# Row softmax on one Trainium2 core: two pairs of input chunks loaded as one DMA each

## The chip, the core and the metric

The kernel runs on one core of a Trainium2 chip. Of the core's engines it uses VectorE (DVE in the profile) for maxima, reciprocals and most of the scaling, ScalarE (ACT) for exponentials and the rest of the scaling, and the 16 DMA engines that move data between HBM and the core's on-chip memory (SBUF, 128 partitions). SyncE (SP) issues the loads and ScalarE's queue issues the stores. The metric is the device time of one execution in microseconds; the kernel before takes 162.3 us (median of 3 runs, 162.19 to 162.3).

## The reference

A softmax over rows of 512 numbers, with temperature 0.5, on 16 x 1024 = 16384 rows of float32 (33.55 MB in, 33.55 MB out):

```python
x_scaled = x / 0.5
x_max = np.max(x_scaled, axis=-1, keepdims=True)
exp_x = np.exp(x_scaled - x_max)
return exp_x / np.sum(exp_x, axis=-1, keepdims=True)
```

## The kernel before

The rows are cut into C = 8 chunks of 2048 rows. In a chunk each of the 128 partitions holds G = 16 consecutive rows, so a chunk is 4 MiB and one partition's part of it is 32 KiB, contiguous in HBM. Everything is done in place in a chunk's tile `xt`. There are six tiles (`BUFS = 6`); chunks 6 and 7 reuse the tiles of chunks 0 and 1.

`load(c)` (line 66) issues a chunk's loads on SyncE. Chunk 0 is loaded as two DMAs, 4 rows a partition and then 12; the others are one DMA each (`LOADS`). The first seven DMAs (chunks 0 to 5) need no free tile and are issued at once; those of chunks 6 and 7 wait until the stores of chunks 0 and 1 have landed. Loads are called from `shift`, but SyncE's own order is simply chunk order.

The compute works on blocks (`BLOCKS`): chunk 0 in three blocks of 4, 4 and 8 rows a partition, chunks 1 to 6 as one block of 16 each, chunk 7 as two of 8; eleven blocks in all. For each block:

- `shift(i)`: VectorE takes the negated maximum of every row (line 74, `negmax`) and doubles it (line 78, `bias`). Line 74 is the first instruction that needs the block's load to have landed.
- `exponentials(i, rows)`: ScalarE computes exp(2x + bias) row by row, with the row's sum (line 86).
- `scale_vector(i)`: VectorE takes the reciprocals of the sums (line 101) and multiplies the first 7/8 of the rows (line 103).
- `scale_scalar(i)`: ScalarE multiplies the remaining rows (line 112).
- `store(i)`: after a chunk's last block, ScalarE issues one DMA for the whole chunk (line 120).

The order on each engine is the program's (`manual_schedule`); nothing is rearranged. The main loop is short:

```python
    for i in range(n):
        if i + 1 < n:
            exponentials(i + 1, rows(i + 1)[0])
        scale_vector(i)
        scale_scalar(i)
        if i + 2 < n:
            shift(i + 2)
        store(i)
        if i + 1 < n:
            exponentials(i + 1, rows(i + 1)[1])
```

On VectorE this makes the sequence: scaling of block i, maximum of block i+2, scaling of block i+1, maximum of block i+3. The maximum of chunk 2 (block 4) thus stands ahead of the scaling of chunk 1 (block 3), whichever is ready first. On ScalarE the store of block i stands after the exponentials of block i+1.

Of the kernel before, what the change touches and what calls it, by code (L numbers as in the profile page):

```python
# [1 line left out]

# [4 lines left out]


@with_exitstack
def kernel(  # L10
    ctx: ExitStack,
    tc: tile.TileContext,
    x: bass.AP,
    out: bass.AP,
):
    nc = tc.nc
    fp32 = mybir.dt.float32
    P = nc.NUM_PARTITIONS
    AX = mybir.AxisListType.X
    EXP = mybir.ActivationFunctionType.Exp  # L20
    COPY = mybir.ActivationFunctionType.Copy
    MAX = mybir.AluOpType.max

    D = x.shape[-1]
    xf = x.flatten_outer_dims()
    of = out.flatten_outer_dims()
    N = xf.shape[0]

    G = 16
    C = N // (P * G)
    assert C * P * G == N
    xr = xf.rearrange("(c p g) d -> c p g d", p=P, g=G)
    outr = of.rearrange("(c p g) d -> c p g d", p=P, g=G)
    WHOLE = [(0, G)]
    LOADS = [[(0, 4), (4, G)]] + [WHOLE] * 7
    BLOCKS = [[(0, 4), (4, 8), (8, G)]] + [WHOLE] * 6 + [[(0, 8), (8, G)]]
    STORES = [WHOLE] * 8  # L40
    BMAX = 16
    BUFS = 6

    data = ctx.enter_context(tc.tile_pool(name="data", bufs=BUFS))
    stats = ctx.enter_context(tc.tile_pool(name="stats", bufs=6))

    ctx.enter_context(tc.manual_schedule())


    warm = stats.tile([P, 1], fp32, name="warm", bufs=1)  # L50
    nc.vector.memset(warm, 0.0)  # L51
    nc.scalar.activation(out=warm, in_=warm, func=EXP)  # L52

    chunks = {}
    blocks = [(c, lo, hi) for c in range(C) for lo, hi in BLOCKS[c]]
    n = len(blocks)
    biases, sums, recips = {}, {}, {}

    def load(c):
        if c < BUFS:  # L60
            chunks[c] = data.tile([P, G, D], fp32, name="xt")
        else:
            chunks[c] = chunks[c - BUFS]
        xt = chunks[c]
        for lo, hi in LOADS[c]:
            nc.sync.dma_start(out=xt[:, lo:hi, :], in_=xr[c][:, lo:hi, :])  # L66

    def shift(i):
        c, lo, hi = blocks[i]
        if c not in chunks:  # L70
            load(c)
        b = hi - lo
        negmax = stats.tile([P, BMAX], fp32, name="negmax")
        nc.vector.tensor_reduce(  # L74
            negmax[:, 0:b], chunks[c][:, lo:hi, :], axis=AX, op=MAX, negate=True
        )
        biases[i] = stats.tile([P, BMAX], fp32, name="bias")
        nc.vector.tensor_scalar_mul(biases[i][:, 0:b], negmax[:, 0:b], 2.0)  # L78

    def exponentials(i, rows):  # L80
        c, lo, hi = blocks[i]
        if i not in sums:
            sums[i] = stats.tile([P, BMAX], fp32, name="sums")
        for g in rows:
            row = chunks[c][:, lo + g, :]
            nc.scalar.activation(  # L86
                out=row,
                in_=row,
                func=EXP,
                bias=biases[i][:, g : g + 1],  # L90
                scale=2.0,
                accum_out=sums[i][:, g : g + 1],
            )


    def scale_vector(i):
        c, lo, hi = blocks[i]
        b = hi - lo
        k = b - b // 8
        recips[i] = stats.tile([P, BMAX], fp32, name="recip")  # L100
        nc.vector.reciprocal(recips[i][:, 0:b], sums[i][:, 0:b])  # L101
        rows = chunks[c][:, lo : lo + k, :]
        nc.vector.tensor_mul(  # L103
            rows, rows, recips[i][:, 0:k].unsqueeze(2).broadcast_to((P, k, D))
        )

    def scale_scalar(i):
        c, lo, hi = blocks[i]
        b = hi - lo
        for g in range(b - b // 8, b):  # L110
            row = chunks[c][:, lo + g, :]
            nc.scalar.activation(  # L112
                out=row, in_=row, func=COPY, scale=recips[i][:, g : g + 1]
            )

    def store(i):
        c, _, end = blocks[i]
        for lo, hi in STORES[c]:
            if hi == end:
                nc.scalar.dma_start(  # L120
                    out=outr[c][:, lo:hi, :], in_=chunks[c][:, lo:hi, :]
                )

    shift(0)
    shift(1)

    def rows(i):
        c, lo, hi = blocks[i]
        cut = hi - lo - (2 if c == 1 else 0)
        return range(cut), range(cut, hi - lo)  # L130

    exponentials(0, rows(0)[0])
# [12 lines that stand above are left out]
# [1 line left out]
_INS = ['x']  # L146
_OUTS = [((16, 1024, 512), 'float32')]


# [23 lines left out]
```

## Time and profile before

| | |
|---|---|
| median of the runs | 162.3 us |
| profiled execution | 162.04 us |
| its span | 160.3 us |
| VectorE busy | 134.6 us (84%), 45 instructions |
| ScalarE busy | 102.2 us (64%), 273 instructions |
| HBM read, written | 33.55 MB, 33.55 MB; 419 GB/s over the span |
| maximum of a whole chunk (line 74) | 8.68 us |
| scaling of a whole chunk (line 103) | 7.62 us |
| chunk store, issue to landing | 22.8 us (median of 8) |
| whole-chunk load, issue to landing | 30.1 us (median of 7) |

A profile line of a group reads: line, engine, operation, output<-input, count, busy time, mean duration of one. In the timeline the first two numbers are start and duration in us; "SPq" and "ACTq" are DMA issues by SyncE and ScalarE. In the list of waits the numbers are total us, number of waits and the longest. In the page's slices each digit is the busy share, in tenths, of one fortieth of the span. A row of DMA issues ends with the size of one and the us from issue to landing. The row of a stretch gives the stretch, its length, the busy time (and instruction count) of VectorE, ScalarE and GpSimd, the TensorE clock (not used here), the DMA engines' busy share and GB/s.

### The profile page before, as it was taken

To read this page: it belongs to the slowest core of one execution; us is meant where nothing else is said; L and a number is where in the kernel's file an instruction comes from. 1 tells how busy PE (TensorE), PEld (TensorE's weight loads), DVE (VectorE), ACT (ScalarE), POOL (GpSimd) and SP (SyncE) were. 2 spreads that over 40 slices of the span, in tenths; PEclk is the share of its full clock that TensorE was granted. 3 is DMA by queue.
4 is the path that set the end of the run, shared out by engine and by line. 5 is a ranking of instruction groups with operands and counts; after the bars stand their busy time and mean duration, and the time that the engine had idled before them with its cause. 6 is when DMAs were issued, how large, how long until landed. Compare 5 with 4: busy or idle time off the path is not lost.

```text
span 160.3 us, 402 instructions
## 1 busy us (share of the span) xinstructions
DVE 134.6 (84%) x45; ACT 102.2 (64%) x273; POOL 0.2 (0%) x4
## 2 busy tenths in 40 slices
DVE  0607999999999999999999999999999999957000
ACT  3071549069989972998199909991899891690000
POOL 0000000000000000000000000000000000000000
DMA  5999999999999999999999999999999999999993
GB/s 180 474 409 491 409 401 483 425 393 452 458 393 401 393 425 474 409 393 499 417 393 474 442 393 468 442 393 442 474 393 417 491 401 401 491 417 401 466 442 139
DMA packets 2450, 67.13 MB, mean 419 GB/s; under 512 B 272, under 2 KB 272, under 8 KB 272
## 3 DMA queue, kind: packets, MB, share of 16 engines
q1 hardware_dynamic: 1296, 33.56, 49.4%
q10 hardware_dynamic: 1152, 33.55, 48.5%
q14 instruction: 2, 0.02, 0.0%
HBM read 33.55 MB, written 33.55 MB: 419 GB/s over the span
## 4 chain that ended last, share of the span: by engine, by line
DVE 80%; DMA 7%; ACT 4%; issue 0%; SPq 0%
DVE negmax L74 42%; DVE xt L103 36%; DMA xt<-in_x_dram 7%; ACT xt L86 4%; DVE bias L78 1%; DVE recip L101 1%; SPq L66 0%
## 5 line engine op out<-in xcount | busy, mean ns | idle before, releaser
L86 ACT ACTIVATE xt<-xt,bias 128x512 f32<-128x512 f32 x128 | 90.4, 708 | 41.5 <-DVE bias L78 40.6
L74 DVE TENSOR_REDUCE negmax<-xt 128x16 f32<-128x8192 f32 (+2 forms) x11 | 69.9, 6353 | 9.5 <-DMA xt<-in_x_dram 9.5
L103 DVE TENSOR_TENSOR xt<-xt,recip 128x7168 f32<-128x7168 f32 (+2 forms) x11 | 62.0, 5637 | 0.4
L86 ACT ACTIVATION_READ_ACCUMULATOR xt<-xt,bias 128x1 f32 x128 | 23.9, 187 | 0.0
L112 ACT ACTIVATE xt<-xt,recip 128x512 f32<-128x512 f32 x15 | 9.9, 707 | 0.0
L101 DVE RECIPROCAL recip<-sums 128x16 f32<-128x16 f32 (+2 forms) x11 | 2.4, 218 | 1.8 <-ACT xt L86 1.8
L78 DVE TENSOR_SCALAR bias<-negmax 128x16 f32<-128x16 f32 (+2 forms) x11 | 1.9, 173 | 0.4
L52 ACT ACT_TABLE_LOAD x1 | 1.3, 1283 | 0.7 <-PEq L157 0.7
L51 DVE MEMSET warm<- 128x1 f32 x1 | 0.1, 59 | 0.8 <-PEq L157 0.8
L52 ACT ACTIVATE warm<-warm 128x1 f32<-128x1 f32 x1 | 0.2, 202 | 0.0
L157 POOL MEMSET const-bfloat16-1.0<- 128x1 bf16 x1 | 0.1, 101 | 0.0
L157 POOL MEMSET const-uint8-127<- 128x1 uint8 x1 | 0.1, 101 | 0.0
L157 POOL MEMSET const-float32-0.0<- 128x1 f32 x1 | 0.1, 98 | 0.2 <-issue 0.2
L157 POOL MEMSET const-float32-1.0<- 128x1 f32 x1 | 0.1, 98 | 0.0
## 6 DMA issues: line engine op xcount, KB each, us to landing
out_dram<-xt ACTq DMA_DIRECT2D x8, 4096.0 KB, 22.8
xt<-in_x_dram SPq DMA_DIRECT2D x7, 4096.0 KB, 30.1
xt<-in_x_dram SPq DMA_DIRECT2D x1, 3072.0 KB, 11.7
xt<-in_x_dram SPq DMA_DIRECT2D x1, 1024.0 KB, 4.8
```

The lines of the kernel that those rows point to most:

```text
L51: nc.vector.memset(warm, 0.0)
L52: nc.scalar.activation(out=warm, in_=warm, func=EXP)
L74: nc.vector.tensor_reduce(negmax[:, 0:b], chunks[c][:, lo:hi, :], axis=AX, op=MAX, negate=True)
L78: nc.vector.tensor_scalar_mul(biases[i][:, 0:b], negmax[:, 0:b], 2.0)
L86: nc.scalar.activation(out=row, in_=row, func=EXP, bias=biases[i][:, g : g + 1], scale=2.0, accum_out=sums[i][:, g : g + 1],)
L101: nc.vector.reciprocal(recips[i][:, 0:b], sums[i][:, 0:b])
L103: nc.vector.tensor_mul(rows, rows, recips[i][:, 0:k].unsqueeze(2).broadcast_to((P, k, D)))
L112: nc.scalar.activation(out=row, in_=row, func=COPY, scale=recips[i][:, g : g + 1])
L157: nc = _bacc.Bacc("TRN2", target_bir_lowering=False, num_devices=1)
```

## The change

Rows are dealt to partitions 32 at a time rather than 16, so that a partition holds 64 KiB of consecutive rows of a pair of chunks; a chunk is one half of a pair's tile. There are four pairs and three pair tiles (`BUFS = 3`), with the fourth pair reusing the first's tile. The first pair is loaded in three DMAs (4, 12 and 16 rows a partition), the second pair (third and fourth chunk) as one DMA, the third pair (fifth and sixth chunk) as one DMA, and the last pair as two DMAs, a chunk each. Stores are still one DMA per chunk, and blocks and the main loop are unchanged. `load(c)` issues those DMAs of the pair that overlap chunk c and have not been issued yet.

```diff
-    xr = xf.rearrange("(c p g) d -> c p g d", p=P, g=G)
-    outr = of.rearrange("(c p g) d -> c p g d", p=P, g=G)
+    H = 2 * G
+    xr = xf.rearrange("(c p g) d -> c p g d", p=P, g=H)
+    outr = of.rearrange("(c p g) d -> c p g d", p=P, g=H)
     WHOLE = [(0, G)]
-    LOADS = [[(0, 4), (4, G)]] + [WHOLE] * 7
+    CHUNKS = [(0, G), (G, H)]
+    PAIR = [(0, H)]
+    LOADS = [[(0, 4), (4, G), (G, H)], PAIR, PAIR, CHUNKS]
     BLOCKS = [[(0, 4), (4, 8), (8, G)]] + [WHOLE] * 6 + [[(0, 8), (8, G)]]
-    STORES = [WHOLE] * 8
+    STORES = [CHUNKS] * 4
-    BUFS = 6
+    BUFS = 3
...
     def load(c):
-        if c < BUFS:
-            chunks[c] = data.tile([P, G, D], fp32, name="xt")
-        else:
-            chunks[c] = chunks[c - BUFS]
-        xt = chunks[c]
-        for lo, hi in LOADS[c]:
-            nc.sync.dma_start(out=xt[:, lo:hi, :], in_=xr[c][:, lo:hi, :])
+        pair, at = c // 2, c % 2 * G
+        if pair not in pairs:
+            if pair < BUFS:
+                pairs[pair] = data.tile([P, H, D], fp32, name="xt")
+            else:
+                pairs[pair] = pairs[pair - BUFS]
+        xt = pairs[pair]
+        for lo, hi in LOADS[pair]:
+            if lo < at + G and hi > at and (pair, lo) not in loaded:
+                loaded.add((pair, lo))
+                nc.sync.dma_start(out=xt[:, lo:hi, :], in_=xr[pair][:, lo:hi, :])
+        chunks[c] = xt[:, at : at + G, :]
...
     def store(i):
         c, _, end = blocks[i]
-        for lo, hi in STORES[c]:
-            if hi == end:
+        pair, at = c // 2, c % 2 * G
+        for lo, hi in STORES[pair]:
+            if hi == at + end:
                 nc.scalar.dma_start(
-                    out=outr[c][:, lo:hi, :], in_=chunks[c][:, lo:hi, :]
+                    out=outr[pair][:, lo:hi, :], in_=pairs[pair][:, lo:hi, :]
                 )
```

More of the change, by code (lines that the diff above doesn't have):

```diff
@@ L52 @@
     nc.scalar.activation(out=warm, in_=warm, func=EXP)
-    chunks = {}
+    pairs, chunks, loaded = {}, {}, set()
     blocks = [(c, lo, hi) for c in range(C) for lo, hi in BLOCKS[c]]
```

## The prediction

> **What bounds the kernel now.** I read the page first: busy times, the DMA line of the slices, the chain that ended last.
>
> ```profile
> DVE 134.6 (84%) x45; ACT 102.2 (64%) x273; POOL 0.2 (0%) x4
> DMA  5999999999999999999999999999999999999993
> DVE 80%; DMA 7%; ACT 4%; issue 0%; SPq 0%
> ```
>
> Two things are full at once. The DMA engines are busy in every slice from the second to the last but one; VectorE carries 80% of the chain. So I ask two questions of the change: does VectorE get a new idle stretch, and if so, do the DMA engines have queued work to cover it at the end? For the first, the list of waits:
>
> ```profile
> DVE negmax L74 <- DMA xt<-in_x_dram: 9.5, 2, 4.8
> DVE recip L101 <- ACT xt L86: 1.8, 1, 1.8
> ACT xt L86 <- DVE bias L78: 40.6, 10, 5.9
> ```
>
> VectorE waits for loads only twice, both times for chunk 0 at the start; ScalarE waits for VectorE and has slack (its ten waits). From 12.82 us to 141.5 us VectorE runs back to back, so any stall put into it there moves all that follows. Its timeline around chunk 2's maximum:
>
> ```profile
> 24.57 8.68 DVE L74 TENSOR_REDUCE negmax<-xt 128x16 f32<-128x8192 f32 x1
> 33.60 3.89 DVE L103 TENSOR_TENSOR xt<-xt,recip 128x3584 f32<-128x3584 f32 x1
> 37.41 8.68 DVE L74 TENSOR_REDUCE negmax<-xt 128x16 f32<-128x8192 f32 x1
> 46.48 7.62 DVE L103 TENSOR_TENSOR xt<-xt,recip 128x7168 f32<-128x7168 f32 x1
> ```
>
> These are chunk 1's maximum, chunk 0's last scaling, chunk 2's maximum (the instruction the change touches) at 37.41, and chunk 1's scaling. When are the loads there? SyncE issues them in order; for the fifth (chunk 3) and the seventh (chunk 5), its timeline gives the issue, and the DMA view of the same window the time to landing:
>
> ```profile
> 2.72 0.59 SPq L66 DMA_DIRECT2D xt<-in_x_dram  x1
> xt<-in_x_dram SPq DMA_DIRECT2D x1, 4096.0 KB, 39.5
> ...
> 3.87 0.44 SPq L66 DMA_DIRECT2D xt<-in_x_dram  x1
> xt<-in_x_dram SPq DMA_DIRECT2D x1, 4096.0 KB, 72.7
> ```
>
> Chunk 3 lands at about 2.72 + 39.5 = 42.2 us, chunk 5 at 3.87 + 72.7 = 76.6. Only loads run up to 44.1 us, when the first store is issued, at this rate (stretches; the last number is GB/s):
>
> ```profile
> 22.50:32.20 9.70, 9.70 (x2) 5.54 (x16) 0.00 (x0) 1.00 1.00 432
> 32.20:42.00 9.80, 9.73 (x5) 8.51 (x25) 0.00 (x0) 1.00 1.00 429
> ```
>
> At 432 GB/s a chunk of 4.19 MB takes 9.71 us, so chunk 2 landed at about 42.2 - 9.7 = 32.5, some 5 us before its use at 37.41. For the second question, the end: ScalarE's last store, and the DMA view from its issue on.
>
> ```profile
> 147.50 0.34 ACTq L120 DMA_DIRECT2D out_dram<-xt  x1
> DMA packets 164, 4.33 MB, mean 338 GB/s; under 512 B 32, under 2 KB 32, under 8 KB 32
> out_dram<-xt ACTq DMA_DIRECT2D x1, 4096.0 KB, 11.9
> ```
>
> 4.33 MB move after that issue, 4.19 of them this store's own. The backlog is some 0.14 MB, plus packets in flight: next to nothing. The last store lands at 147.5 + 11.9 = 159.4, and the span ends at 160.3. VectorE's chain and the DMA engines are level at the end, so neither has slack to give.
>
> **What the Trainium skill says.** "DMA: Bandwidth & Descriptors", section "Why a DMA increments its semaphore by 16 and not by 1": only the full count says that all data has landed, and an intermediate value does not tell which bytes have. So the first half of one big load can't be used early. The trace agrees as far as it goes: chunk 0's first megabyte, a DMA of its own, lets line 74 start at 5.55, and the 3 MB beside it release the next maximum only at 12.82. Same page, "Queues, rings and completion order": each DMA engine takes turns between queues packet by packet. Here, with 32 KiB pieces in both queues, loads moved 8.26 and stores 6.32 MB from 42.3 to 76.5 us (the first store's bytes start late, behind queued loads). Same page, "Where 436 GB/s comes from": a ceiling of 435 GB/s; the 432 measured is at it, so larger pieces have no rate to win. Same page, "Latency and other measured facts", the entry on row pitch: HBM copies still ran at 207 GB/s with a 512 KiB pitch a partition, against 214 with a padded one. The change makes the pitch 64 KiB; no run here shows it, and I put its cost at zero.
>
> **The change, part by part.**
>
> 1. *Layout.* Rows are dealt to partitions 32 at a time. Each piece of a store or single load is still 32 KiB (8 and 24 KiB for chunk 0's two loads), only at a doubled pitch in HBM. VectorE and ScalarE see the same shapes, so every compute instruction keeps its duration. SBUF: 3 x 64 KiB replaces 6 x 32 KiB. Cost 0 (bounds: a rate gain of 3 in 435, under 1%; a loss is a rival below).
>
> 2. *Two load issues fewer on SyncE.* Each took about 0.4 to 0.6 us, at 2 to 4 us, with loads already queued for 40 us. Hidden by those loads; without that cover it would gain 1 us.
>
> 3. *Chunks 2 and 3 as one DMA.* The bytes ahead are the same (chunks 0 and 1), only loads run until 44.1, so the pair is complete when chunk 3 was: 42.2 to 42.3. Chunk 2's maximum, at 37.41, now waits until 42.29 (VectorE started 0.02 us after chunk 0's landings). New stall: 42.29 - 37.41 = **4.88 us**. Behind it on VectorE, in order, stand chunk 2's bias, and chunk 1's reciprocal and scaling (46.48 becomes 51.36), although chunk 1 is ready. ScalarE's exponentials of chunk 2 go from 46.33 to 51.2; chunk 0's store at 44.11 is ahead of that wait and doesn't move; chunk 1's goes from 58.97 to 63.85. From here VectorE is again back to back, so all later stores move by 4.88: the last from 147.50 to 152.38.
>
> 4. *Chunks 4 and 5 as one DMA.* Chunk 4's maximum started at 70.65; now 70.65 + 4.88 = 75.53. Two bounds for the pair's landing. If queues share bytes equally as before: 76.55, chunk 5's time; stall 1.0. If they alternate by packets, a 64 KiB load piece against a 32 KiB store piece, loads get two thirds of 432 = 288 GB/s, and 8.39 MB from 42.3 take at most 29.1 us: 71.4, no stall. I take the second, from the skill's statement. Then the first store is late instead: in the worst case 144 GB/s for it until 71, landing near 72 rather than 68.2. Late next is the load of chunk 6, which reuses its place (issued 68.16 before, now near 72; it took 28 us and lands by 100), needed at 103.88 + 4.88 = 108.8. Chunk 7's load waits for chunk 1's store (87.4 before, near 87 to 90 now), plus 28 gives 118; needed at 125.4. No cost; without these 7 to 8 us of cover it would be 4.
>
> 5. *The end.* The last store is issued at 152.38. Loads were over at about 116, and stores come one per 16.6 us against 9.7 us of transfer, so the stall turns up as idle DMA time ahead of the last two or three stores. The last store then meets an empty queue. How long does it take? Above: chunk 0's first load, on an empty queue, took 4.8 us for 1.05 MB, of which 2.43 are transfer at 432: overhead 2.37, so 9.71 + 2.37 = 12.1. Below: its first bytes moved 1.0 us after issue (the DMA view of the first 2.2 us), plus 9.71 and about 0.4 from the last packet to the landing: 11.1. I take 11.5[...]. Against 11.9 before that returns 0.4 (bounds: 0.8 returned, 0.2 more).
>
> Sum: 160.3 + 4.88 - 0.4 = 164.8 span; the profiled execution took 162.04, 1.74 around its span, which gives 166.5. The runs' median, 162.3, is 0.26 above the profiled one: **166.8 us**, +2.8%. Bounds of this case: 166.4 to 167.4.
>
> **The rivals.**
>
> *A second stall at chunk 4.* If 64 KiB pieces are served as two packets, sharing stays equal, pair 2 lands at 76.55, and VectorE loses another 1.0: 167.8. For it: chunk 5 really landed at 76.55. Against: the packet rule. Chance 0.12.
>
> *A slower memory pattern, or reuse waits that span a whole pair.* With the 64 KiB pitch 1.5% below 432 GB/s, the pair lands 0.6 later (1.5% of 41 us) and pair 2 perhaps 1 later: 168.4. If chunk 6's load waited for both stores of its pair, issue slips from 72 to about 88, landing to about 111 against 108.8, and chunk 7 behind it to some 129 against 125.4: 3 to 4 more, 170.5. Against: partial loads of one tile release their readers separately in the trace. Together 0.06.
>
> *The stall is hidden by backlog, no change.* The end is set by bytes queued rather than by VectorE. Place: the DMA queue at the last store's issue. Price: 0 if the backlog is worth 4.9 us or more, 4.88 x 432 = 2.1 MB. Measured: some 0.14 MB plus packets in flight, and stores later by 4.88 leave less. 162.3. Its faster variant, larger pieces landing the pair by 37.41, needs 8.39 MB in 37.41 - 22.5 = 14.9 us, 563 GB/s, above the ceiling. Chance 0.04.
>
> **How the numbers follow.** The main case has 0.78; its bounds, with 0.2 to 0.4 for another run's median, are 166.0 to 167.6. The second stall reaches 168.4. Range 166.0 to 168.4 holds the main case and that rival, about 0.88 less the tails of both. A change of 0.2% is about what a measurement here can tell from none. Faster 0.02, same 0.02 (the hidden case), slower 0.96.
>
> **What would show it.** In the profile after: VectorE waits for the load three times, the new wait 4.9 us before chunk 2's maximum at 42.3; VectorE and ScalarE durations unchanged; the last store issued near 152.4 and landing 11.1 to 12.1 later; lowered digits in the DMA line in the last quarter; no wait at chunk 4. I am wrong if the pair lands well before or after 42.3, if loads move at another rate than 432 GB/s, if a fourth wait for loads appears, or if the last store is still queued behind others.

## The result and the profile after

The changed kernel takes 165.95 us (median of 6 runs, 165.81 to 166.12) against 162.3 us (6 runs beside it, 162.19 to 162.64): a ratio of 1.0223, 95% interval 1.021 to 1.0236. The forecast was 166.8 with a range of 166.0 to 168.4. Direction and mechanism held; the time fell 0.05 us below the range. What follows shows which part of the sum was too large.

The page of the changed kernel, the same lines as were shown of before, with the span ahead of them:

```profile
span 164.3 us, 398 instructions
DVE 134.7 (82%) x45; ACT 102.2 (62%) x273; POOL 0.2 (0%) x4
DMA  5999995997989899698999989999999688985885
DVE 63%; DMA 24%; ACT 4%; SPq 1%; issue 0%
```

Busy times have not changed (134.6 and 102.2 before), and DMA's share of the chain went from 7% to 24%, as the chain now runs through the load that VectorE waits for at chunk 2 rather than the one at chunk 0. The DMA line has lost its solid row of nines, but its digits need care. The profile counts a packet whole in the slice in which it starts. The 64 KiB packets of the joined loads take about 2.4 us each (64 KiB at a sixteenth of 432 GB/s), so with slices of 4.1 us a 5 can stand beside a slice that was credited with too much. While only loads run, the engines are in fact as full as before and as fast (432 and 429 GB/s then as now):

```profile
22.50:32.20 9.70, 9.70 (x2) 5.44 (x16) 0.00 (x0) 1.00 1.00 432
32.20:42.00 9.80, 5.13 (x4) 8.60 (x25) 0.00 (x0) 1.00 0.99 429
```

After the first slice only the lowered digits of the last quarter are idle time; they are taken up below. The waits of the changed kernel:

```profile
DVE negmax L82 <- DMA xt<-in_x_dram: 14.3, 3, 4.9
```

Three waits for loads where there were two, and 14.3 us in place of 9.5: the new one is 4.9 us. VectorE's timeline shows where it is (the bracket is the idle time before the instruction, and what ended it):

```profile
33.51 3.89 DVE L111 TENSOR_TENSOR xt<-xt,recip 128x3584 f32<-128x3584 f32 x1
42.29 8.69 DVE L82 TENSOR_REDUCE negmax<-xt 128x16 f32<-128x8192 f32 x1 [4.89 <-DMA xt<-in_x_dram]
51.37 7.62 DVE L111 TENSOR_TENSOR xt<-xt,recip 128x7168 f32<-128x7168 f32 x1
...
75.53 8.68 DVE L82 TENSOR_REDUCE negmax<-xt 128x16 f32<-128x8192 f32 x1
```

Chunk 2's maximum starts at 42.29 in place of 37.41, chunk 1's scaling at 51.37 in place of 46.48, chunk 4's maximum at 75.53 with nothing waited for. Everything from there on is later by the same amount. At the end, ScalarE's last store, and the DMA view of the window in which it is issued:

```profile
152.38 0.34 ACTq L129 DMA_DIRECT2D out_dram<-xt  x1
out_dram<-xt ACTq DMA_DIRECT2D x1, 4096.0 KB, 11.1
```

Issued 4.88 us later than before, it took 11.1 us to land where it took 11.9. So 4.88 - 0.8 = 4.1 us between the two profiled executions (162.04 and 166.12). Idle DMA time appeared where it was looked for, ahead of the last stores (stretches; the last number is GB/s):

```profile
126.00:130.00 4.00, 3.96 (x3) 4.00 (x12) 0.00 (x0) 1.00 0.68 295
130.00:134.00 4.00, 3.97 (x3) 3.53 (x10) 0.00 (x0) 1.00 0.92 393
...
150.00:154.00 4.00, 2.30 (x1) 0.00 (x0) 0.00 (x0) 1.00 0.31 131
```

Taken together, the first two rows are some 1.6 us short of 432 GB/s, and the third is 2.8 us short. The second figure is again coarse, since packets that started before 150 us are not in it: by the start and duration of each packet the engines idle 1.7 us between 128 and 132 us, and 2.5 us just before the last store's first packet at 153.22. In the kernel before they idle nowhere between 4 us and that kernel's last packet.

### The profile page after: what moved, and what is told of

The parts are those of the page before. It is cut to its first block, busy times and chain, and to the rows that moved or that the text cites. A ratio compares the mean times of both kernels' runs of the same rounds, so it can differ in the third digit from the quotient of the medians.

```text
span 164.3 us, 398 instructions
## 1 busy us (share of the span) xinstructions
DVE 134.7 (82%) x45; ACT 102.2 (62%) x273; POOL 0.2 (0%) x4
## 4 chain that ended last, share of the span: by engine, by line
DVE 63%; DMA 24%; ACT 4%; SPq 1%; issue 0%
DVE negmax L82 32%; DVE xt L111 30%; DMA xt<-in_x_dram 24%; ACT xt L94 4%; DVE bias L86 1%; SPq L73 1%; DVE recip L109 1%
## 5 line engine op out<-in xcount | busy, mean ns | idle before, releaser
L82 DVE TENSOR_REDUCE negmax<-xt 128x16 f32<-128x8192 f32 (+2 forms) x11 | 69.9, 6352 | 14.3 <-DMA xt<-in_x_dram 14.3
## 6 DMA issues: line engine op xcount, KB each, us to landing
xt<-in_x_dram SPq DMA_DIRECT2D x1, 3072.0 KB, 11.6
```

Source lines behind the costliest of these rows:

```text
L82: nc.vector.tensor_reduce(negmax[:, 0:b], chunks[c][:, lo:hi, :], axis=AX, op=MAX, negate=True)
```

## The experiments

The theory: the whole loss is VectorE's wait for the second half of a joined load, less a fixed return at the end. The rivals: the doubled row pitch costs transfer rate; the 64 KiB pieces cost something of their own; each joined load costs a share.

### The layout without joined loads

```diff
-    LOADS = [[(0, 4), (4, G), (G, H)], PAIR, PAIR, CHUNKS]
+    LOADS = [[(0, 4), (4, G), (G, H)], CHUNKS, CHUNKS, CHUNKS]
```

> The pair layout with every chunk loaded by its own DMA (32 KiB pieces at a 64 KiB pitch in HBM). Theory (the loss is VectorE's wait for the second half of a joined load): no wait at chunk 2, last store issued at 147.5, 162.3 us, within 0.3. Rival (the doubled pitch costs transfer rate): loads below 432 GB/s and a good part of the 3.65 us stays, 163.5 to 166.

Measured: 162.5 us, ratio to before 1.0013 (1.0007 to 1.002), some 0.2 us. The list of waits is back to two:

```profile
DVE negmax L82 <- DMA xt<-in_x_dram: 9.2, 2, 4.8
```

The pitch and the rewritten indexing are not the loss. The interval leaves 0.1 to 0.3 us for them; whether that is the pitch wasn't followed further, as it is at the bound of what can be measured.

### One joined load at a time

The first variant joins chunks 2 and 3 only, the second chunks 4 and 5 only.

```diff
-    LOADS = [[(0, 4), (4, G), (G, H)], PAIR, PAIR, CHUNKS]
+    LOADS = [[(0, 4), (4, G), (G, H)], PAIR, CHUNKS, CHUNKS]
```
```diff
-    LOADS = [[(0, 4), (4, G), (G, H)], PAIR, PAIR, CHUNKS]
+    LOADS = [[(0, 4), (4, G), (G, H)], CHUNKS, PAIR, CHUNKS]
```

> Pair layout, only chunks 2 and 3 joined in one DMA; chunks 4 and 5 load separately. Theory: the whole loss is here, wait of 4.9 us at chunk 2, last store issued at 152.4, 165.9 us. Rival (each joined load costs about half): 164.1.

> Pair layout, only chunks 4 and 5 joined. In the changed kernel this pair landed at 72.5, before its use at 75.5; here the use is at 70.65, as no earlier stall covers it. Theory: a wait of 1.8 us at chunk 4, last store issued at 149.3, landing 11.1 later on an empty queue (160.4 against 159.4): 163.3 us. Rival (each joined load costs about half): 164.1. Rival (joining this pair is free wherever it stands): 162.3.

Measured: chunks 2 and 3 joined, 165.8 us, ratio 1.022 (1.0206 to 1.0233), the whole loss. Chunks 4 and 5 joined, 162.47 us, ratio 1.0023 (1.0007 to 1.0039). Not each load a half, then: one costs everything and the other nearly nothing. The second number refutes my 163.3, and the fault was in reading: I had taken the landing of the first store in the changed kernel (72.5) for that of the pair. The pair's issue and time to landing, in the changed kernel and then in the variant:

```profile
2.80 0.45 SPq L73 DMA_DIRECT2D xt<-in_x_dram  x1
xt<-in_x_dram SPq DMA_DIRECT2D x1, 67.2
```

```profile
3.23 0.50 SPq L73 DMA_DIRECT2D xt<-in_x_dram  x1
xt<-in_x_dram SPq DMA_DIRECT2D x1, 66.7
...
70.43 8.68 DVE L82 TENSOR_REDUCE negmax<-xt 128x16 f32<-128x8192 f32 x1
```

It lands at 2.80 + 67.2 = 70.0, and in the variant at 3.23 + 66.7 = 69.9, half a microsecond before chunk 4's maximum at 70.43. No wait, by a thin margin. Of its 15 runs, 13 lie between 162.29 and 162.89 and two at 163.58 and 163.85; a pair landing late in those two would explain them, but only one execution was profiled, and that stays open.

### Joined completion, but 32 KiB pieces

The layout of before, and one DMA that carries two chunks as two 32 KiB pieces for each partition:

```diff
-    xr = xf.rearrange("(c p g) d -> c p g d", p=P, g=H)
-    outr = of.rearrange("(c p g) d -> c p g d", p=P, g=H)
+    xr = xf.rearrange("(c p g) d -> c p g d", p=P, g=G)
+    outr = of.rearrange("(c p g) d -> c p g d", p=P, g=G)
...
+                if hi - lo == H:
+                    nc.sync.dma_start(
+                        out=xt.rearrange("p (c g) d -> p c (g d)", c=2),
+                        in_=xr[2 * pair : 2 * pair + 2].rearrange(
+                            "c p g d -> p c (g d)"
+                        ),
+                    )
...
```

The single loads and the stores, not shown, are indexed by chunk again to match.

> The layout of before (32 KiB pieces, pitch 32 KiB), but chunks 2 and 3, and chunks 4 and 5, each in one DMA of two pieces a partition. Theory: the same wait of 4.9 us at chunk 2, since it comes from the joined completion and not from the piece size; with equal pieces loads and stores share the DMA engines equally, so the pair of chunks 4 and 5 lands at about 76.5 against a use at 75.5: a further wait of 1.0 us; last store issued at 153.4, 166.9 to 167.2 us. Rival (the 64 KiB pieces are the cost): 162.3 to 163.5.

Measured: 166.2 us, ratio 1.0243 (1.023 to 1.0256). The wait at chunk 2 is there without any 64 KiB piece, so the piece size is not what costs. The further wait at chunk 4 did not come. The pair of chunks 4 and 5, and the two maxima:

```profile
2.73 0.48 SPq L74 DMA_DIRECT2D xt<-in_x_dram  x1
xt<-in_x_dram SPq DMA_DIRECT2D x1, 8192.0 KB, 72.6
...
42.20 8.69 DVE L92 TENSOR_REDUCE negmax<-xt 128x16 f32<-128x8192 f32 x1 [4.85 <-DMA xt<-in_x_dram]
...
75.45 8.68 DVE L92 TENSOR_REDUCE negmax<-xt 128x16 f32<-128x8192 f32 x1
```

It lands at 2.73 + 72.6 = 75.3, just ahead of its use at 75.45 and 1.2 us sooner than I expected; why sooner stays open. Against the 70.0 us of the changed kernel this is what piece size does here: it decides which queue gets the larger share of the DMA engines. Bytes by queue (q1 loads, q10 stores) while loads and the first stores overlap, first the changed kernel from 48 to 66 us, then this one from 49.5 to 66:

```profile
q1 hardware_dynamic: 79, 5.18, 66.3%
q10 hardware_dynamic: 80, 2.62, 33.7%
```

```profile
q1 hardware_dynamic: 111, 3.64, 51.1%
q10 hardware_dynamic: 104, 3.41, 47.8%
```

79 load packets against 80 store packets, two to one in bytes; then 111 against 104, nearly equal in bytes. The profile lists each piece, 64 or 32 KiB, as one packet, and by these counts the two queues take turns piece by piece.

### The delay alone, in the kernel before

Extra VectorE work ahead of chunk 2's maximum, in the kernel before, with its loads untouched. The reductions read a zeroed scratch tile, and nothing uses their result. The list `[4, 4, 1]` (sizes in units of 512 elements) is the longest delay; the others are `[1]`, `[2]` and `[4]`.

```diff
...
         b = hi - lo
+        if i == 4:
+            for rows_idle in [4, 4, 1]:
+                nc.vector.tensor_reduce(
+                    idlemax[:, 0:rows_idle], idle[:, 0:rows_idle, :], axis=AX, op=MAX
+                )
         negmax = stats.tile([P, BMAX], fp32, name="negmax")
```

> The kernel before, with one extra VectorE reduction of 512 elements a partition (about 0.6 us) ahead of chunk 2's maximum. Theory (the last store of the kernel before stood about 0.8 us behind queued bytes, so the first 0.8 us of any delay is free): last store issued 0.6 later, landing not later, 162.3 us within 0.25. Rival (the last store met an empty queue, every us of VectorE counts): 162.9.

> The kernel before with one extra VectorE reduction of 2 x 512 elements a partition (about 1.1 us) ahead of chunk 2's maximum. Theory (the first 0.8 us of delay is free): 0.3 us over the kernel before, 162.5 to 162.6. Rival (every us counts once the last store meets an empty queue, nothing is returned): 1.1 us over it.

> The kernel before with one extra VectorE reduction of 4 x 512 elements a partition (about 2.2 us) ahead of chunk 2's maximum. Theory (the first 0.8 us of delay is free): 1.4 us over the kernel before, last store 11.1 us from issue to landing. Rival (a further return grows with the delay, since the changed kernel's median rose by 3.65 and not by 4.1): about 1.0 over it. Rival (nothing returned): 2.2 over it.

> The kernel before, with three extra VectorE reductions of 9 x 512 elements in all (about 5.0 us) ahead of chunk 2's maximum, loads and pieces untouched. Theory: as the changed kernel, 5.0 less 0.8, 166.1 us, last store 11.1 us from issue to landing. Rival (part of the changed kernel's loss comes from its loads): clearly less than 165.9. Rival (no return at the end): 167.3.

The changed kernel was run once more beside the second and third:

> The changed kernel once more, beside the two above. Theory (stall of 4.88 less 0.8): 4.1 us over the kernel before; from the first comparison of medians: 3.65 over it.

"Delay" is the issue of the last store less 147.50, from one profile each; that issue varies somewhat between executions (it stood at 147.27 with the layout alone), so the delay is good to about 0.2 us. "Rise" is the median less that of the kernel before in the same comparison, and "returned" is the delay less the rise.

| kernel | delay us | rise us | ratio (95%) | returned us |
|---|---|---|---|---|
| 1 x 512 | 0.60 | 0.05 | 1.0002 (0.9994 to 1.001) | 0.55 |
| 2 x 512 | 1.13 | 0.15 | 1.0011 (1.0004 to 1.0017) | 0.98 |
| 4 x 512 | 2.16 | 1.15 | 1.0071 (1.0057 to 1.0085) | 1.01 |
| 9 x 512 | 5.15 | 4.58 | 1.0281 (1.0268 to 1.0295) | 0.57 |
| changed kernel | 4.88 | 3.65 | 1.0223 (1.021 to 1.0236) | 1.23 |
| changed kernel again | 4.76 | 3.77 | 1.0232 (1.0218 to 1.0246) | 0.99 |

The last stores of the first three rows:

```profile
148.10 0.34 ACTq L128 DMA_DIRECT2D out_dram<-xt  x1
out_dram<-xt ACTq DMA_DIRECT2D x1, 4096.0 KB, 11.6
```

```profile
148.63 0.34 ACTq L128 DMA_DIRECT2D out_dram<-xt  x1
out_dram<-xt ACTq DMA_DIRECT2D x1, 4096.0 KB, 11.1
```

```profile
149.66 0.34 ACTq L128 DMA_DIRECT2D out_dram<-xt  x1
out_dram<-xt ACTq DMA_DIRECT2D x1, 4096.0 KB, 11.1
```

By the medians the first half microsecond is free (in its one profile the last store lands at 148.10 + 11.6 = 159.7, 0.3 later than before), and from about 1 us on each microsecond of VectorE counts whole. 11.1 us is what a 4 MiB store took on an empty queue in all of these kernels but the first: 9.7 for 4.19 MB at 432 GB/s, and so 1.4 of start and completion. In the profiles the return is 11.9 - 11.1 = 0.8 us, as I had expected, in every kernel from 1.1 us of delay on; it neither vanishes nor grows with the delay. Between medians it scatters from 0.57 to 1.23. So a pure delay reproduces the changed kernel's loss, with one loose end: the longest delay costs 0.8 us more than the changed kernel. 0.3 to 0.4 of that is its longer delay. Another 0.4 lies outside the span (166.78 - 164.6 = 2.2 us, against 166.12 - 164.3 = 1.8), in all four of its runs, and I have no cause for it.

### VectorE given slack

Both kernels with two rows more of each whole chunk scaled on ScalarE:

```diff
-        k = b - b // 8
+        k = b - b // 4
...
-        for g in range(b - b // 8, b):
+        for g in range(b - b // 4, b):
```

> The changed kernel with a quarter of the rows scaled on ScalarE in place of an eighth. VectorE's scaling of a whole chunk falls by 2 rows, 7.62 to about 6.55 us, so it makes up 1.07 us a chunk after the stall, some 5 us by the last store. Theory (the loss is VectorE's lateness, DMA work is unchanged): the end falls back to what the DMA engines need, 162.2 to 162.8 us. Rival (large pieces or the pitch cost DMA time): stays at 165 or above.

> The kernel before with a quarter of the rows scaled on ScalarE. Theory (the DMA engines are full from 1.7 us on and set the end once VectorE has slack): 162.0 to 162.3 us, the last stores waiting in the queue, longer from issue to landing than 11.9. Rival (VectorE's chain alone sets the end): 5 or more us faster.

Measured: the changed kernel 162.66 us, ratio to before 1.0027 (1.0017 to 1.0038); the kernel before with the same edit 162.79, ratio 1.0033 (1.0021 to 1.0046). With slack on VectorE the joined loads cost nothing that can be told from this pair, although the wait at chunk 2 is longer than ever. Both lie some 0.5 us above the kernel before; the second thereby missed its forecast of 162.0 to 162.3, and where that half microsecond comes from was not followed. Waits of the first:

```profile
DVE negmax L82 <- DMA xt<-in_x_dram: 15.9, 3, 6.5
```

Its last store is issued at 145.79 and takes 14.3 us, because it now queues. In the other, issue and landing of the last store:

```profile
141.44 0.34 ACTq L120 DMA_DIRECT2D out_dram<-xt  x1
out_dram<-xt ACTq DMA_DIRECT2D x1, 4096.0 KB, 18.0
```

Issued 6 us earlier than in the kernel before, it lands no earlier (141.44 + 18.0 = 159.4). The DMA engines are the floor, at about 162.3 us: no variant's median went below that of the kernel before.

## Why the prediction was right and where it was wrong

**What bounds the kernel.** Right, and shown from both sides: a last store issued 6 us earlier brings nothing, and delays beyond about 1 us count whole.

**Steps 1 and 2, layout and issues.** Near enough: the layout alone costs some 0.2 us (0.1 to 0.3), where 0 was put. The two issues fewer came only together with joined loads, so no run shows their share; that loads ran at 432 GB/s without a gap agrees with their being hidden.

**Step 3, the stall.** Forecast 42.29 and 4.88 us; measured 42.29 and 4.88. The variant with this pair alone carries the whole loss, and the variant with 32 KiB pieces shows that joined completion is the cause. One phrase there was loose: chunk 1 was not ready at the start of the stall. ScalarE finished its exponentials at about 46, inside the stalled maximum, so by these times issuing chunk 1's scaling first would not have filled the gap; no run tried it.

**Step 4, the other pair.** Right: at most 71.4 was forecast for its landing, 70.0 was measured, and the shares of the two queues are two to one. The rule it rested on, that an engine takes turns between queues packet by packet, is the Trainium skill's ("DMA: Bandwidth & Descriptors", section "Queues, rings and completion order"). That one piece counts as one packet is not in that section, which speaks of some 9 to 17 descriptors to a packet; the forecast assumed it, and the 79 packets against 80 bear it out. The first store landed at about 72.5 as the price (68.1 before), and chunk 6's load was issued just after. That no wait arose rested on the first stall having moved chunk 4's use to 75.53; without it the margin is only half a microsecond.

**Step 5, the end.** This is the step that failed, in size. It bounded the last store on an empty queue by 11.1 and 12.1, and took 11.5; it took 11.1 in every stalled kernel from 1.1 us of delay on. The upper bound was carried over from chunk 0's load, and its overhead of 2.4 us is not that of a store (1.4). I also called the backlog at the last store's issue "next to nothing", having seen 0.14 MB, which is 0.3 us when spread over 16 engines. But a backlog of whole packets isn't spread. Of the 164 packets in the line shown there 32 are small and 128 are the last store's own, so four packets of the store before started only after 147.50; each holds one engine for 1.2 us (32 KiB at a sixteenth of 432 GB/s), and the last store lands when its last engine is done. In the kernel before, the 16 engines took up the last store between 148.37 and 149.38 us; in the changed kernel, with nothing ahead of it, between 153.22 and 153.37. From its issue the last engine thus began 0.9 us sooner, close to the 0.8 us of the return. Half of that return was in the sum, and the missing 0.4 us is one half of the miss.

**The step to the median.** This failed too, and is the other 0.4. I added 0.26 because the profiled execution of before lay that far below its median; the profiled one of the changed kernel lay 0.17 above its own. The offset belonged to one execution and was no property of both kernels. Together 0.4 + 0.43 account for 166.8 - 165.95 = 0.85. Put another way, the return taken was 0.4 and the measured one is 0.8 between the two profiles and about 1.0 to 1.2 between medians. The range's lower end had counted the main case's bounds too tightly for that.

**The rivals.** The second stall did not occur even with equal sharing, by 0.1 us. The pitch is refuted as a cause of more than 0.3 us. The hidden case failed as argued: about 1 us of backlog hid about 1 us, not 4.9.

## What to carry to other kernels

Joining two loads delays the first to the landing of the second; compare that landing with the first use, load by load, since the same edit cost 3.5 us at one pair and next to nothing at the other. Where an in-order engine and the DMA engines are level at the end, a stall costs its length less what the last transfer had been queued, and that queue includes the packets in flight: it ends with the engine that comes free last. When a sum ends in a profiled execution, don't carry its distance from the median over to the other kernel.

## What was not expected of the hardware

A piece of a transfer is the unit in which the two DMA queues take turns, 79 load packets of 64 KiB against 80 store packets of 32 KiB in the same 18 us. So the piece size sets the shares, and it moved the landing of the same 8 MiB from 75.3 us (32 KiB pieces) to 70.0 (64 KiB pieces), while the total rate in these stretches was nearly the same (427 and 433 GB/s). The direction was in the forecast; that it would hold so exactly, piece by piece at this size, was not.
